# In each weight chunk, all products with the high part first, then those with the low part

## The chip, the cores and the metric

The kernel runs on one core of a Trainium2 chip. The time is the device time of one execution in microseconds (us): three runs of the kernel before gave 1134.96, 1135.42 and 1135.75, so the median is 1135.42. One more execution was profiled; its own time was 1134.29, and its span from first to last instruction 1132.6.

## The reference

One layer on x of 256 tokens by 2048 channels: RMS norm, one wide input projection (2048 by 18,544), a Mamba-2 branch (causal convolution, chunked scan, gated group norm), a sparse-attention branch (index scores, top 64 keys of each query, softmax attention with 16 heads of 128), a projection of each branch back to 2048, merging by sigmoid gates, one output projection, the residual sum and a final norm. In its core:

```
proj = rmsnorm(x) @ w_in
y_m = ssd_branch(z, xbc, dt, ...)          # scan over chunks of 64 tokens
y_a = dsa_branch(q, k, v, gate, qi, ki, wi)
merged = g_m * (y_m @ w_branch[:2048]) + g_a * (y_a @ w_branch[2048:])
out = rmsnorm(x + merged @ w_out)
```

Nearly all of the arithmetic lies in the three weight matrices.

## The kernel before, in words

The weights come in 192 chunks of 128 by 2048 float32 (1 MB each), in the order in which they are used. For each chunk `fetch` issues one DMA on SyncE into a `raw` buffer, ScalarE copies it to `hi` in the reduced float32 format of TensorE (fp32r; line 130), and VectorE computes `lo = raw - hi` (line 131). There are three buffers each of raw, hi and lo, and the chunk two ahead of the one in use is fetched while one is consumed, so a new `hi` or `lo` can be written only when TensorE has finished with the chunk three earlier. The activations are split in the same way.

A product of a weight and an activation is then three products: high by high, high by low, low by high. There are two kinds of units.

- T units (`gemm_t`, 46 after the start, two chunks each) hold the weight still and stream the activations. A chunk has 8 blocks of 128 rows and two column blocks. `high` streams 512 columns (high and low activations side by side), `low` streams the 256 high ones. `chunk_t` goes through the 8 blocks: two `high`, two `low`, and so on. A flag, `lo_last`, makes it all `high` first, then all `low`; only the two units at the very start (`acc_start`) set it, since their data come in pieces.
- N units (`gemm_n`, four chunks each) hold the activations still and stream 512 weight columns, for each of two token blocks: three products for each of 4 blocks of rows (lines 202, 203, 204).

Between chunks `tick` lets earlier work go on that needs small matrix products on TensorE: `prs` (sums for a norm), `prt` and `pcb` (a broadcast, and C times B of the scan), `px`, `py`, `pi` (index scores, four tiles of PSUM, `pi0` to `pi3`), `pl` (attention logits) and `po` (values). In the scan part, groups g = 0 to 3, `u` and `c` are the convolution's tiles, `bc` its result on ScalarE (line 406), `E` the decay matrices (relu at line 427, exp at 428), `dgy` a diagonal (line 483) for which GpSimd raises `ss` to a power (line 480). In the attention part `qT` is the scaled query block (lines 189 and 194).

The program text doesn't fix the order on each engine: the framework schedules the instructions by its own estimates of their times, and each engine then executes its list strictly in that order. PSUM tiles of the small products come from a pool of four.

Of the kernel before, what the change touches and what calls it, by code (L numbers as in the profile page):

```python
# [21 lines left out]
KB = 16  # L22
# [62 lines left out]
def block_kernel(ctx, tc, W, w0, xT, xn, par, gbias, nf, out):  # L85
    nc = tc.nc
    mm = nc.tensor.matmul
# [10 lines left out]
    def acc_tile(name):  # L98

        return pacc.tile([P, 2, 512], F32, tag="acc", name=name)  # L100
# [13 lines left out]
    def tick():  # L114
        state["done"] += 1
        while True:
            due = [p for p in pending if p[0] <= state["done"]]
            if not due:
                return
            for p in due:  # L120
                pending.remove(p)
                p[1]()

    def w_tiles():
        return (wraw.tile([P, 2048], F32, tag="raw", name="raw"),
                whi.tile([P, 2048], F32R, tag="hi", name="hi"),
                wlo.tile([P, 2048], F32R, tag="lo", name="lo"))

    def split(hi, lo, raw):
        nc.scalar.activation(hi, raw, AF.Copy)  # L130
        nc.vector.tensor_sub(lo, raw, hi.bitcast(F32))  # L131
# [15 lines left out]
    def next_chunk():  # L147
        while len(ready) < 1 + AHEAD and state["chunk"] < NCHUNK - 4:
            fetch()
        return ready.pop(0)  # L150

    def chunk_t(acc, hi, lo, half, ks, ax, lo_last=False):

        hv = hi.rearrange("p (k b c) -> p k b c", k=8, b=2)
        lv = lo.rearrange("p (k b c) -> p k b c", k=8, b=2)

        def high(k, cb):
            kk = half * 8 + k
            mm(acc[:, cb, :], hv[:, k, cb], ax[:, kk].rearrange("p b t -> p (b t)"), start=kk == 0, stop=False,  # L159
               skip_group_check=True)  # L160

        def low(k, cb):
            kk = half * 8 + k
            mm(acc[:, cb, 0:T], lv[:, k, cb], ax[:, kk, 0, :], start=False, stop=kk == KB - 1,  # L164
               skip_group_check=True)

        for part_ks in ([ks] if lo_last else [[k] for k in ks]):
            for f in (high, low):
                for k in part_ks:
                    for cb in range(2):  # L170
                        f(k, cb)

    def gemm_t(ax):

        assert UNITS[state["unit"]][0] == "T"
        state["unit"] += 1
        acc = acc_tile("acc_t")
        for half in range(2):
            hi, lo = next_chunk()
            chunk_t(acc, hi, lo, half, range(8), ax)  # L180
            if half == 0:
                tick()
        return acc
# [9 lines left out]
        evict_sum(out, acc)  # L193
        nc.vector.tensor_mul(out, out, rbc2)

    def chunk_n(acc, hi, lo, q, tb, ah, al, c=slice(0, 512)):
        hv = hi.rearrange("p (k c) -> p k c", k=4)
        lv = lo.rearrange("p (k c) -> p k c", k=4)
        ts = slice(tb * P, tb * P + P)
        for k in range(4):  # L200
            kk = q * 4 + k
            mm(acc[:, c], ah[:, kk, ts], hv[:, k, c], start=kk == 0, stop=False)  # L202
            mm(acc[:, c], al[:, kk, ts], hv[:, k, c], start=False, stop=False)  # L203
            mm(acc[:, c], ah[:, kk, ts], lv[:, k, c], start=False, stop=kk == KB - 1)  # L204

    def gemm_n(ah, al):

        assert UNITS[state["unit"]][0] == "N"
        state["unit"] += 1
        both = acc_tile("acc_n")  # L210
        acc = [both[:, tb, :] for tb in range(2)]
        for q in range(4):
            hi, lo = next_chunk()
            for tb in range(2):
                chunk_n(acc[tb], hi, lo, q, tb, ah, al)
            if q < 3:
                tick()
        return acc


    part = const.tile([P, NPAR], F32, name="part")
# [8 lines left out]
    xx = acts.tile([P, KB, 2, T], F32R, name="xx")  # L230
# [4 lines left out]
    k0, k1 = PIECES[0]  # L235
# [8 lines left out]
    acc_start = [acc_tile(f"acc_start{u}") for u in range(2)]  # L244
    for k0, k1 in PIECES:
        ks = slice(k0, k1)
        if k0 % 8 == 0:
            wt = [w_tiles() for u in range(2)]
        ws = slice(256 * (k0 % 8), 256 * (k0 % 8) + 256 * (k1 - k0))
        if k0 > 0:  # L250
            nc.sync.dma_start(xraw[:, ks, :], xTv[:, ks, :])
        for u in range(2):
            nc.sync.dma_start(wt[u][0][:, ws], W[2 * u + k0 // 8][:, ws])
        for k in range(k0, k1):
            g = part[:, PN + k:PN + k + 1]
            nc.scalar.activation(xh[:, k, :], xraw[:, k, :], AF.Copy, scale=g)
            nc.vector.scalar_tensor_tensor(xl[:, k, :], xraw[:, k, :], g, xh[:, k, :].bitcast(F32),
                                           ALU.mult, ALU.subtract)
        for u in range(2):
            raw, hi, lo = wt[u]  # L260
            split(hi[:, ws], lo[:, ws], raw[:, ws])
        for u in range(2):
            raw, hi, lo = wt[u]
            chunk_t(acc_start[u], hi, lo, k0 // 8, range(k0 % 8, k0 % 8 + k1 - k0), xx, True)
    state["unit"], state["chunk"] = 2, 4
    ssm = ExitStack()
    grp = ssm.enter_context(tc.tile_pool(name="grp", bufs=1))
# [6 lines left out]
    raw, hi, lo = w_tiles()  # L274
# [6 lines left out]
    hv = hi[:, :nw].rearrange("p (k c) -> p k c", c=112)  # L281
    lv = lo[:, :nw].rearrange("p (k c) -> p k c", c=112)
# [44 lines left out]
    m0, dt, al, R, rmask = (d2[:, i, :] for i in range(5))  # L327
# [175 lines left out]
    def project_v(j, out):  # L503
        acc = gemm_n(xh, xl)
        for tb in range(2):
            nc.scalar.activation(out[:, tb, :], acc[tb], AF.Copy, scale=rn[:, tb:tb + 1])
# [12 lines left out]
    for g in range(4):  # L519
# [18 lines left out]
        for a in range(2):  # L538
            acc = gemm_t(xx)
# [40 lines left out]
    for j in range(4):  # L580
        acc = gemm_t(xx)
# [35 lines left out]
    for j in range(4):  # L617
        js = slice(512 * j, 512 * j + 512)
        acc = gemm_n(xh, xl)
        tick()  # L620
        if j == 0:
            assert not pending
            select()
            ssm.close()
            late = ctx.enter_context(tc.tile_pool(name="late", bufs=1))
            big = ctx.enter_context(tc.tile_pool(name="big", bufs=1))
            merged = late.tile([P, 2, D], F32, name="merged")
            phase = ExitStack()
            tmp = phase.enter_context(tc.tile_pool(name="att", bufs=2))
        sg = tmp.tile([P, 2, 512], F32, tag="sg", name="sgm")  # L630
        gates(acc, 512 * j, sg)
        acc = gemm_n(yh, yl)
        for tb in range(2):
            nc.vector.tensor_mul(merged[:, tb, js], acc[tb], sg[:, tb, :])
        tick()
# [48 lines left out]
    for j in range(8):  # L684
        kq = []
        for name in ("kT", "qT"):
            acc = gemm_t(xx)
# [15 lines left out]
        acc = gemm_t(xx)  # L703
# [7 lines left out]
    for j in range(4):  # L711
        acc = gemm_n(xh, xl)
# [21 lines left out]
    for j in range(4):  # L734
        js = slice(512 * j, 512 * j + 512)
        acc = gemm_n(yh, yl)
# [19 lines left out]
    for j in range(4):  # L756
# [3 lines left out]
        if j < 3:  # L760
# [4 lines left out]
            acc = gemm_n(mh, ml)  # L765
# [9 lines left out]
    for tb in range(2):  # L775
        r = rf[:, tb:tb + 1]

        nc.vector.tensor_reduce(r, sf[:, tb, 0:3], axis=mybir.AxisListType.X, op=ALU.add)
        nc.vector.tensor_scalar(r, r, 1.0 / D, EPS, ALU.mult, ALU.add)

        n = 512 if tb == 0 else 256
        xs = tmp.tile([P, 512], F32, tag="mt", name="xs")
        for i in range(512 // n):
            acc = acc_tile("acc_last")[:, 0, :]
            c = slice(n * i, n * i + n)
            for q in range(4):
                chunk_n(acc, *ready[q], q, tb, mh, ml, c)
            ps = sf[:, tb, 3 + i:4 + i]
            residual(acc[:, c], 1536 + n * i, 1536 + n * i + n, tb, xr[:, tb, c], ps)

            nc.vector.tensor_mul(xs[:, c], x1[:, tb, 1536 + n * i:1536 + n * i + n], nfb[:, 1536 + n * i:1536 + n * i + n])
            nc.gpsimd.tensor_scalar(r, ps, 1.0 / D, r, ALU.mult, ALU.add)
        nc.gpsimd.tensor_tensor(r, r, mhalf[:, 0:1], op=ALU.pow)
        for i, js in enumerate(slice(512 * i, 512 * i + 512) for i in range(4)):
            o = x1[:, tb, js] if i < 3 else xs
            if i == 1:
                nc.scalar.activation(o, o, AF.Copy, scale=r)
            else:
                nc.vector.tensor_scalar(o, o, r, None, ALU.mult)
            (nc.sync, nc.scalar)[i % 2].dma_start(outv[:, tb, js], o)  # L800
# [54 lines left out]
```

## Time and profile before

| what | value |
|---|---|
| median of three runs | 1135.42 us |
| profiled execution: its time, its span | 1134.29 us, 1132.6 us |
| TensorE busy | 1122.6 us (99%), 5906 matmul records |
| TensorE weight loads busy | 956.8 us (84%) |
| VectorE, ScalarE busy | 779.9 us (69%), 560.3 us (49%) |
| mean granted TensorE clock | 0.998 of full speed |

PE is TensorE, PEld its weight loads (which overlap the products), DVE VectorE, ACT ScalarE, POOL GpSimd, SP SyncE. A matmul's record lasts longer than the distance to the next one, since matmuls are pipelined: what a matmul costs is read from the distance between the starts. A float32 matmul that isn't of the reduced format stands in the trace as two records.

### The profile page before, as it was taken

The page shows a single profiled execution, that of the slowest core. Times are in us where ns is not written, and L with a number is a line of the kernel's source. Part 1 is how long each engine was busy: PE and PEld are TensorE (multiplying, and loading weights), DVE is VectorE, ACT ScalarE, POOL GpSimd, SP SyncE. Part 2 cuts the span into 40 slices and gives each one's busy share as a digit, 9 for nine tenths or more (in the row PEclk, how much of TensorE's full clock was granted, in tenths as well). Part 3 has the DMA queues.
Part 4 walks back from the last instruction along what each step waited for, and adds up shares of the span by engine and source line. Part 5 has one row for each costly group of instructions (what it writes and reads, how often), then busy time and mean ns, then how long its engine had stood idle before and what let it go on. Part 6 is the DMA issues. An engine that isn't in the chain of part 4 may idle for free.

```text
span 1132.6 us, 14323 instructions
## 1 busy us (share of the span) xinstructions
PE 1122.6 (99%) x5906; PEld 956.8 (84%) x5906; DVE 779.9 (69%) x995; ACT 560.3 (49%) x532; POOL 8.8 (1%) x24
## 2 busy tenths in 40 slices
PE   9999999999999999999999999999999999999997
PEld 8888888888888888888888888888888888888886
DVE  6688897879777854454447767877678454889663
ACT  6647675748454433433335454555445444333441
POOL 0000000000000000000000000000000000000000
PEclk9999999999999999999999999999999999999999
DMA  8956555554535655655555454545545567465652
GB/s 294 338 181 229 186 203 176 196 206 150 193 141 187 212 196 187 202 204 207 186 186 186 149 190 183 185 144 192 186 155 181 195 201 271 172 220 186 212 197 75
DMA packets 34113, 219.08 MB, mean 193 GB/s; under 512 B 3744, under 2 KB 3968, under 8 KB 9088
## 3 DMA queue, kind: packets, MB, share of 16 engines
q1 hardware_dynamic: 31392, 209.42, 52.2%
q10 hardware_dynamic: 2656, 8.75, 2.3%
q8 instruction: 46, 0.75, 0.3%
q14 instruction: 19, 0.16, 0.0%
HBM read 215.96 MB, written 2.13 MB: 193 GB/s over the span
## 4 chain that ended last, share of the span: by engine, by line
PE 98%; DMA 1%; ACT 0%; DVE 0%; POOLq 0%; DVEq 0%; issue 0%; POOL 0%
PE acc_t L159 30%; PE acc_t L164 15%; PE acc_n L203 15%; PE acc_n L202 15%; PE acc_n L204 15%; PE acc_start L159 1%; PE py L457 1%; PE acc_last L204 1%; PE acc_last L203 1%; PE acc_last L202 1%; DMA raw<-W 1%; PE pl L650 1%; PE po L678 1%; PE pi L567 1%; PE acc_start L164 1%; PE pl L649 0%
## 5 line engine op out<-in xcount | busy, mean ns | idle before, releaser
L131 DVE TENSOR_TENSOR lo<-raw,hi 128x2048 fp32r<-128x2048 f32 (+2 forms) x197 | 437.7, 2222 | 239.8 <-ACT hi L130 237.3
L130 ACT ACTIVATE hi<-raw 128x2048 fp32r<-128x2048 f32 (+2 forms) x197 | 366.3, 1861 | 455.2 <-PE acc_n L203 222.0
L159 PE MATMUL acc_t<-xx,hi 128*128 128x512 f32 x1472 | 466.6, 398 | 0.0
L164 PEld LDWEIGHTS acc_t<-xx,lo 128*128 128x128 f32 x1472 | 276.3, 188 | 65.1
L164 PE MATMUL acc_t<-xx,lo 128*128 128x256 f32 x1472 | 289.8, 278 | 0.0
L159 PEld LDWEIGHTS acc_t<-xx,hi 128*128 128x128 f32 x1472 | 225.0, 189 | 2.6 <-issue 1.7
L202 PE MATMUL acc_n<-hi,xx 128*128 128x512 f32 x480 | 186.9, 389 | 0.0
L203 PE MATMUL acc_n<-hi,xx 128*128 128x512 f32 x480 | 186.9, 389 | 0.0
L204 PE MATMUL acc_n<-lo,xx 128*128 128x512 f32 x480 | 186.8, 389 | 0.0
L203 PEld LDWEIGHTS acc_n<-hi,xx 128*128 128x128 f32 x480 | 90.1, 188 | 18.8 <-issue 0.3
L204 PEld LDWEIGHTS acc_n<-lo,xx 128*128 128x128 f32 x480 | 90.1, 188 | 18.7
L202 PEld LDWEIGHTS acc_n<-hi,xx 128*128 128x128 f32 x480 | 90.1, 188 | 18.5
L202 PE MATMUL acc_n<-hi,yh 128*128 128x512 f32 x256 | 99.6, 389 | 0.0
L203 PE MATMUL acc_n<-hi,yl 128*128 128x512 f32 x256 | 99.6, 389 | 0.0
L204 PE MATMUL acc_n<-lo,yh 128*128 128x512 f32 x256 | 99.6, 389 | 0.0
L204 PEld LDWEIGHTS acc_n<-lo,yh 128*128 128x128 f32 x256 | 48.1, 188 | 10.0
L203 PEld LDWEIGHTS acc_n<-hi,yl 128*128 128x128 f32 x256 | 48.1, 188 | 10.0
L202 PEld LDWEIGHTS acc_n<-hi,yh 128*128 128x128 f32 x256 | 48.1, 188 | 9.9
L670 DVE STREAM_TRANSPOSE pT<-le 32x192 f32<-32x192 f32 x128 | 47.3, 370 | 1.9
L404 DVE SCALAR_TENSOR_TENSOR c<-u,part,c 128x255 f32<-128x255 f32 (+2 forms) x72 | 30.4, 479 | 0.5
L729 DVE STREAM_TRANSPOSE mT<-merged 32x256 f32<-32x256 f32 x64 | 27.9, 436 | 0.8
L159 PE MATMUL acc_start<-xx,hi 128*128 128x512 f32 x64 | 16.6, 396 | 1.2 <-ACT hi L130 1.0
(199 smaller groups left out, 732.1 us busy)
## 6 DMA issues: line engine op xcount, KB each, us to landing
raw<-W SPq DMA_DIRECT2D x188, 1024.0 KB, 4.8
acb<-adr ACTq DMA_DIRECT2D x4, 1024.0 KB, 4.6
raw<-W SPq DMA_DIRECT2D x6, 512.0 KB, 7.7
xt<-xn SPq DMA_DIRECT2D x2, 1024.0 KB, 5.5
gb<-gbias SPq DMA_DIRECT2D x8, 256.0 KB, 3.5
xr<-xn ACTq DMA_DIRECT2D x4, 512.0 KB, 5.2
xraw<-xT SPq DMA_DIRECT2D x3, 512.0 KB, 6.1
raw<-W SPq DMA_DIRECT2D x4, 256.0 KB, 4.5
```

The lines of the kernel that those rows point to most:

```text
L130: nc.scalar.activation(hi, raw, AF.Copy)
L131: nc.vector.tensor_sub(lo, raw, hi.bitcast(F32))
L159: mm(acc[:, cb, :], hv[:, k, cb], ax[:, kk].rearrange("p b t -> p (b t)"), start=kk == 0, stop=False, skip_group_check=True)
L164: mm(acc[:, cb, 0:T], lv[:, k, cb], ax[:, kk, 0, :], start=False, stop=kk == KB - 1, skip_group_check=True)
L202: mm(acc[:, c], ah[:, kk, ts], hv[:, k, c], start=kk == 0, stop=False)
L203: mm(acc[:, c], al[:, kk, ts], hv[:, k, c], start=False, stop=False)
L204: mm(acc[:, c], ah[:, kk, ts], lv[:, k, c], start=False, stop=kk == KB - 1)
L404: nc.vector.scalar_tensor_tensor(c[:, b, sh:], u[:, b, :T - sh], wv[3 - sh], c[:, b, sh:], ALU.mult, ALU.add)
L457: mm(py[r, cb, sb * P:], xdt[:, sb, 64 * h:64 * h + 64], M[a][:, 2 * cb + i, (0, T)[sb]:(T, 384)[sb]], start=cb == 0 and sb == 0, stop=cb ...
L567: mm(pi[2 * cb + i][:, cs[tb]], qi[r, cb, tb * P:tb * P + P], kidx[r, :(P, T)[tb]], start=tb == 0, stop=tb == 1, skip_group_check=True, ti ...
L670: nc.vector.transpose(t[sj, :, :, si], lv[si, :, :, sj])
L729: nc.vector.transpose(tv[sn, :, :, si], mv[si, :, :, sn])
```

## The change

`chunk_t` loses the flag, and every T chunk has its 16 `high` first and then its 16 `low`. `chunk_n` can do one part alone, and `gemm_n` calls it four times for each chunk: high part for both token blocks, then low part for both. The last unit calls `chunk_n` without a part; there the order inside each call is 8 high, 4 low. Products and their number are the same.

```diff
-        for part_ks in ([ks] if lo_last else [[k] for k in ks]):
-            for f in (high, low):
-                for k in part_ks:
-                    for cb in range(2):
-                        f(k, cb)
+        for f in (high, low):
+            for k in ks:
+                for cb in range(2):
+                    f(k, cb)
...
-        for k in range(4):
-            kk = q * 4 + k
-            mm(acc[:, c], ah[:, kk, ts], hv[:, k, c], start=kk == 0, stop=False)
-            mm(acc[:, c], al[:, kk, ts], hv[:, k, c], start=False, stop=False)
-            mm(acc[:, c], ah[:, kk, ts], lv[:, k, c], start=False, stop=kk == KB - 1)
+        if part != "low":
+            for k in range(4):
+                kk = q * 4 + k
+                mm(acc[:, c], ah[:, kk, ts], hv[:, k, c], start=kk == 0, stop=False)
+                mm(acc[:, c], al[:, kk, ts], hv[:, k, c], start=False, stop=False)
+        if part != "high":
+            for k in range(4):
+                kk = q * 4 + k
+                mm(acc[:, c], ah[:, kk, ts], lv[:, k, c], start=False, stop=kk == KB - 1)
...
-            for tb in range(2):
-                chunk_n(acc[tb], hi, lo, q, tb, ah, al)
+            for part in ("high", "low"):
+                for tb in range(2):
+                    chunk_n(acc[tb], hi, lo, q, tb, ah, al, part=part)
```

Because the framework schedules by its estimates, other instructions move too. On TensorE, in the unit with the second block of index scores, this stands before (`lo_2705` is the end of a chunk, `hi_2779` the start of the next; "waits" names the engines on which an instruction waits):

```order
L164 MATMUL acc_t_2820<-xx_89,lo_2705 128x256 x2
L490 MATMUL prt_2859<-dgy_2747,ones_80 128x128 [waits Activation_49]
L490 MATMUL prt_2859<-dgy_2747,ones_80 128x128
L567 MATMUL pi0_2870<-kidx_408,qi_2816 128x128 [waits DVE_49,Activation_49]
L567 MATMUL pi1_2871<-kidx_408,qi_2816 128x128 [waits Activation_49]
L567 MATMUL pi0_2870<-kidx_408,qi_2816 128x256
L567 MATMUL pi1_2871<-kidx_408,qi_2816 128x256
L567 MATMUL pi2_2872<-kidx_408,qi_2816 128x128 [waits Activation_49]
L567 MATMUL pi2_2872<-kidx_408,qi_2816 128x256
L159 MATMUL acc_t_2820<-xx_89,hi_2779 128x512
L567 MATMUL pi3_2873<-kidx_408,qi_2816 128x128 [waits DVE_49,PE_49]
L567 MATMUL pi3_2873<-kidx_408,qi_2816 128x256
```

and this in the changed kernel (its lines 572 and 495 are 567 and 490 of before):

```order
L159 MATMUL acc_t_2820<-xx_89,hi_2704 128x512 x16
L164 MATMUL acc_t_2820<-xx_89,lo_2705 128x256 x16
L495 MATMUL prt_2859<-dgy_2747,ones_80 128x128 [waits PE_49,Activation_49]
L495 MATMUL prt_2859<-dgy_2747,ones_80 128x128 [waits Activation_49]
L572 MATMUL pi0_2870<-kidx_408,qi_2816 128x128 [waits DVE_49]
L572 MATMUL pi1_2871<-kidx_408,qi_2816 128x128 [waits Activation_49]
L572 MATMUL pi0_2870<-kidx_408,qi_2816 128x256
L572 MATMUL pi1_2871<-kidx_408,qi_2816 128x256
L572 MATMUL pi2_2872<-kidx_408,qi_2816 128x128 [waits Activation_49]
L572 MATMUL pi3_2873<-kidx_408,qi_2816 128x128 [waits Activation_49]
L572 MATMUL pi2_2872<-kidx_408,qi_2816 128x256
L572 MATMUL pi3_2873<-kidx_408,qi_2816 128x256
```

The one `high` product that stood between the products of `pi2` and those of `pi3` has moved behind the group, which is now in one piece and in the order of the other three groups.

On ScalarE, ahead of `bc` of group 1, this stands before, from the eviction of the unit (`u`) on:

```order
L188 ACTIVATE u_1138<-acc_t_1032 128x512 [waits PE_49]
L130 ACTIVATE hi_1156<-raw_1155 128x2048 [waits DMAHW1_49]
L427 ACTIVATE E_1260<-E_1260 128x1536 [waits DVE_49]
L401 ACTIVATE c_1141<-u_1138,part_78 128x256 [waits DVE_49]
L401 ACTIVATE c_1141<-u_1138,part_78 128x256
L428 ACT_TABLE_LOAD
L428 ACTIVATE E_1260<-E_1260 128x1536 [waits Activation_49]
L130 ACTIVATE hi_1203<-raw_1202 128x2048 [waits DMAHW2_49,PE_49]
L406 ACT_TABLE_LOAD [waits DVE_49]
L406 ACTIVATE bc_1142<-c_1141 128x512 [waits Activation_49]
L483 ACTIVATE dgy_1199<-ident_84,ss_1196 128x128 [waits Pool_49]
L483 ACTIVATE dgy_1199<-ident_84,ss_1196 128x128
```

and this in the changed kernel, behind the same `u` (whose row is left off):

```order
L432 ACTIVATE E_1260<-E_1260 128x1536 [waits DVE_49]
L432 ACTIVATE E_1266<-E_1266 128x1536 [waits DVE_49]
L130 ACTIVATE hi_1203<-raw_1202 128x2048 [waits DMAHW2_49,PE_49]
L406 ACTIVATE c_1141<-u_1138,part_78 128x256 [waits DVE_49]
L406 ACTIVATE c_1141<-u_1138,part_78 128x256
L488 ACTIVATE dgy_1199<-ident_84,ss_1196 128x128 [waits Pool_49]
L488 ACTIVATE dgy_1199<-ident_84,ss_1196 128x128
L433 ACT_TABLE_LOAD
L433 ACTIVATE E_1260<-E_1260 128x1536 [waits Activation_49]
L433 ACTIVATE E_1266<-E_1266 128x1536 [waits Activation_49]
L411 ACT_TABLE_LOAD [waits DVE_49]
L411 ACTIVATE bc_1142<-c_1141 128x512 [waits Activation_49]
```

Both halves of `E` and the diagonal `dgy` now stand ahead of `bc`; the split `hi_1156` has moved ahead of `u`.

On TensorE, the product that reads `bc` stands in the third unit after `bc`'s own. Before:

```order
L159 MATMUL acc_t_1154<-xx_89,hi_1101 128x512 x2
L164 MATMUL acc_t_1154<-xx_89,lo_1102 128x256 x2
L159 MATMUL acc_t_1272<-xx_89,hi_1156 128x512 [waits PE_49,Activation_49]
L159 MATMUL acc_t_1272<-xx_89,hi_1156 128x512
L412 MATMUL pcb_1255<-bc_1142 128x256 [waits Activation_49]
L413 MATMUL pcb_1255<-bc_1142 128x128
```

and in the changed kernel:

```order
L164 MATMUL acc_t_1154<-xx_89,lo_1102 128x256 x16
L159 MATMUL acc_t_1272<-xx_89,hi_1156 128x512 [waits Activation_49]
L159 MATMUL acc_t_1272<-xx_89,hi_1156 128x512 x9
L417 MATMUL pcb_1255<-bc_1142 128x256 [waits Activation_49]
L418 MATMUL pcb_1255<-bc_1142 128x128
L159 MATMUL acc_t_1272<-xx_89,hi_1156 128x512 x6
```

`pcb` stood behind 2 `high` products of its unit and now stands behind 10. Groups 2 and 3 have the same moves; in group 0 `pcb` stays at the end of a chunk.

## Rows read from the trace of the kernel before

**Rows 1.** The page: shares of the span in the chain that ended last.
```profile
PE 98%; DMA 1%; ACT 0%; DVE 0%; POOLq 0%; DVEq 0%; issue 0%; POOL 0%
```
**Rows 2.** Timeline, PE, units of the start (start us, us, engine, line, xcount).
```profile
23.91 2.00 PE L159 MATMUL acc_start<-xx,hi 128*128 128x512 f32 x8
25.75 1.12 PE L164 MATMUL acc_start<-xx,lo 128*128 128x256 f32 x8
26.71 2.00 PE L159 MATMUL acc_start<-xx,hi 128*128 128x512 f32 x8
```
**Rows 3.** Timeline, PE, starts of two chunks of T units, two chunks between them.
```profile
578.48 0.63 PE L159 MATMUL acc_t<-xx,hi 128*128 128x512 f32 x2
...
595.20 0.63 PE L159 MATMUL acc_t<-xx,hi 128*128 128x512 f32 x2
```
**Rows 4.** Timeline, PE, last unit: 40 matmuls, then 90, between these rows.
```profile
1104.07 0.39 PE L204 MATMUL acc_last<-lo,xx 128*128 128x512 f32 x1
...
1113.13 0.28 PE L202 MATMUL acc_last<-hi,xx 128*128 128x256 f32 x1
...
1123.93 0.28 PE L202 MATMUL acc_last<-hh,xx 128*128 128x256 f32 x1
```
**Rows 5.** Timeline, PE, first and second group of index scores.
```profile
319.14 1.58 PE L567 MATMUL pi<-kidx,qi 64*128 64x128 f32 x16
320.65 0.73 PE L159 MATMUL acc_t<-xx,hi 128*128 128x512 f32 x2
...
332.44 1.57 PE L567 MATMUL pi<-kidx,qi 64*128 64x128 f32 x12
...
335.23 0.50 PE L159 MATMUL acc_t<-xx,hi 128*128 128x512 f32 x1
```
**Rows 6.** Timeline, ACT, DVE and PE, one block of attention logits (idle before <-releaser).
```profile
667.68 1.92 ACT L130 ACTIVATE hi<-raw 128x2048 fp32r<-128x2048 f32 x1 [3.65 <-PE acc_t L159]
669.63 2.29 DVE L131 TENSOR_TENSOR lo<-raw,hi 128x2048 fp32r<-128x2048 f32 x1 [3.28 <-ACT hi L130]
672.56 0.69 DVE L194 TENSOR_TENSOR qT<-qT,rbc 128x512 f32<-128x512 f32 x1
673.01 0.40 PE L164 MATMUL acc_t<-xx,lo 128*128 128x256 f32 x2
673.31 0.49 PE L649 MATMUL pl<-kT,qT 128*128 128x128 f32 x2
673.63 0.60 PE L650 MATMUL pl<-kT,qT 128*128 128x256 f32 x2
674.07 0.38 PE L649 MATMUL pl<-kT,qT 128*128 128x128 f32 x2
674.29 0.60 PE L650 MATMUL pl<-kT,qT 128*128 128x256 f32 x2
```
**Rows 7.** Timeline, PE, DVE, POOL and ACT, around bc of group 1.
```profile
135.11 0.50 PE L477 MATMUL prs<-ones,sz 128*128 128x1 f32 x4
141.13 0.63 PE L159 MATMUL acc_t<-xx,hi 128*128 128x512 f32 x2
...
137.24 0.14 DVE L479 TENSOR_SCALAR ss<-prs 128x2 f32<-128x2 f32 x1
...
137.46 1.08 POOL L480 TENSOR_TENSOR ss<-ss,mhalf 128x2 f32<-128x2 f32 x1 [92.12 <-DVE ss L479]
...
135.80 1.49 ACT L428 ACTIVATE E<-E 128x1536 f32<-128x1536 f32 x1
139.12 1.28 ACT L406 ACT_TABLE_LOAD   x1
140.41 0.64 ACT L406 ACTIVATE bc<-c 128x512 f32<-128x512 f32 x1
140.95 0.68 ACT L483 ACTIVATE dgy<-ident,ss 128x128 f32<-128x128 f32 x2
```

More of the change, by code (lines that the diff above doesn't have):

```diff
@@ L150, in next_chunk, with chunk_t @@
         return ready.pop(0)
-    def chunk_t(acc, hi, lo, half, ks, ax, lo_last=False):
+    def chunk_t(acc, hi, lo, half, ks, ax):
         hv = hi.rearrange("p (k b c) -> p k b c", k=8, b=2)
@@ L194, in evict_t, with chunk_n @@
         nc.vector.tensor_mul(out, out, rbc2)
-    def chunk_n(acc, hi, lo, q, tb, ah, al, c=slice(0, 512)):
+    def chunk_n(acc, hi, lo, q, tb, ah, al, c=slice(0, 512), part=None):
         hv = hi.rearrange("p (k c) -> p k c", k=4)
@@ L263, in block_kernel @@
             raw, hi, lo = wt[u]
-            chunk_t(acc_start[u], hi, lo, k0 // 8, range(k0 % 8, k0 % 8 + k1 - k0), xx, True)
+            chunk_t(acc_start[u], hi, lo, k0 // 8, range(k0 % 8, k0 % 8 + k1 - k0), xx)
     state["unit"], state["chunk"] = 2, 4
```

## The prediction

> **What bounds the kernel now.** I read the page's shares of the chain that ended last first. The chain is TensorE for 98% [rows 1]. So the time is the sum of the distances between TensorE's matmul starts, and only two things can move it: what a matmul costs by its place in the order, and the few places where TensorE stands still for a small product. ScalarE and VectorE matter only where their order makes a small product late. Next I read the timeline of TensorE for the distances, and then, around each kind of small product, the timeline of the engines that feed it.
>
> I call a product of 512 columns with the high part H and one of 256 columns with the low part L. After the start there are 46 T units of two chunks, so 92 T chunks, each with 16 H and 16 L: 1472 of each.
>
> **Term 1: the order of H and L, 92 chunks.** Before, a chunk is 8 times H H L L. One chunk starts at 578.48 and the third after it at 595.20, so a chunk takes 16.72 / 3 = 5.573 us [rows 3]. The new order is in the trace already, in pieces of half the length: the units of the start run 8 H and then 8 L. The H take 25.75 - 23.91 = 1.84 us, the L 0.96, together 2.80 [rows 2]. Two such pieces would be 5.60. But a chunk will have one long piece of each and not two short ones. In a long run the distances settle: 40 matmuls of 512 columns in the last unit take 1113.13 - 1104.07 = 9.06 us, which is 0.2265 each, and 90 of 256 columns take 10.80, which is 0.120 each [rows 4]. The first 8 H after L are thus 1.84 - 8 x 0.2265 = 0.03 above the settled rate, and they pay that once in a chunk. So a chunk will take 1.84 + 8 x 0.2265 + 0.96 + 8 x 0.120 = 5.57 us. These rows are rounded to 0.01 and leave a gain of 0 to 0.015 for each chunk; I take 0.007 from the middle. Times 92 this is -0.6 us. The bounds: at the settled rates throughout, 16 x (0.2265 + 0.120) = 5.544, it would be -2.7 us; if the slow H after a run of L grow with the run's length (0.03 more in each chunk), about +2. I take -0.6, since the trace shows both run lengths next to it.
>
> [...]
>
> N units: all their products have 512 columns, in either order, and the settled 0.2265 holds for all three kinds [rows 4]. I cost that edit at nothing. The first token block's sum is now complete only 4 products before the second's instead of 12. VectorE and ScalarE read it outside TensorE's path, since the next unit writes the other accumulator.
>
> **Term 2: one split group of index scores.** The first group of `pi` takes from 319.14 to 320.65, 1.51 us. In the second, one H stands between `pi2` and `pi3`, and the group takes from 332.44 to 335.23, 2.79 us, with that one H of 0.23 in it [rows 5]. The price of the split is 2.79 - 1.51 - 0.23 = 1.05 us. The new order has the group in one piece: -1.05 us. The third and fourth groups were whole already. Bounds: 0 if `pi3` then waits for its buffer, and -1.05.
>
> **Term 3: attention logits, 8 times.** `pl` waits for `qT`. `qT` ends at 672.56 + 0.69 = 673.25 and `pl` starts at 673.31 [rows 6]. The two L ahead of it started at 673.01, and two L take 0.24 (8 take 0.96 [rows 2]), so `pl` could have started at 673.25: 0.06 late. Its first pair takes 673.63 - 673.31 = 0.32, the same pair of the second head 674.29 - 674.07 = 0.22: the late weight load costs another 0.10. Together 0.16 us, 8 times, 1.3 us.
>
> What makes `qT` late is a buffer. The split `hi` at 667.68 waited 3.65 us for TensorE's last H of a chunk; `lo` at 669.63 waited for that `hi`; `qT` stands behind that `lo` on VectorE [rows 6]. In the new order the last H of a chunk is followed by 16 L (1.92 us) instead of 2, so this `hi` can start about 1.7 us earlier. The `lo` has its own buffer to wait for, freed by the last L at the chunk's end, which is about 667.9. It starts there instead of at 669.63, and `qT` is ready at about 671.5. What is late next is nothing: `pl` follows the chunk at once. -1.3 us; bounds 0 and -1.3.
>
> **Term 4: `pcb` of groups 1 to 3.** ScalarE's new list puts both `E` and `dgy` ahead of `bc`, and TensorE's list puts `pcb` 8 H later. I follow it with group 1's rows [rows 7]. `dgy` needs `ss`, and that needs `prs`, whose place on TensorE stays: 135.11 + 0.50 = 135.61. In the old list VectorE came to `ss` only at 137.24, in the new one `ss` stands before a `lo`, so VectorE takes it at once, at 135.65. GpSimd starts 137.46 - 137.24 = 0.22 after that and takes 1.08: 136.95. The eviction, the two relus, the split and `c` are done by about 136.3 by their durations, so ScalarE waits for GpSimd. Then `dgy` 0.68, a table load 1.28, two exps of 1.49, a table load 1.28, `bc` 0.64: 6.86 us, so `bc` is there at 143.81. TensorE starts its unit at 141.13 and reaches `pcb` after 10 H: 1.84 + 2 x 0.2265 = 2.29, so at 143.42. It waits 0.4 us, in three groups 1.2 us. What is queued behind `pcb` is the whole of TensorE, so all of it counts. Bounds: 0, if GpSimd's rough duration is too long by 0.4; and if everything added to the list (a relu and an exp of 1.49 and `dgy`, 3.7 us) came out in full against the 8 H (1.85) and the old slack of 0.5 (`bc` ended at 141.05, and `pcb` stood two H after 141.13), 1.3 us three times, +4. I take +1.2.
>
> Everything else hides. The splits were ready ahead of need, and L is needed 3.6 us later in each chunk than before, while `hi` buffers come free earlier. The DMAs and their number stay. ScalarE has fewer table loads. In the attention part a `lo` now stands ahead of the softmax on VectorE, which delays `po`'s input by about 2 us, but `po` comes a unit and a half later on TensorE.
>
> **The sum** is -0.6 - 1.05 - 1.3 + 1.2 = -1.75 us, from 1134.29 to 1132.54 for the profiled execution. That execution was 1.13 below the median of the runs, so for the median I say 1135.42 - 1.75 = 1133.7.
>
> **Rivals.**
> - `bc` is in time (Term 4 is zero). For it: my chain rests on GpSimd's span, which the profile calls rough, and the framework put `pcb` where its estimates have `bc` ready; before, `bc` came 0.5 ahead. Against it: the durations add up to a wait. The time: 1135.42 - 2.95 = 1132.5, faster.
> - The early release buys nothing (Terms 2 and 3 vanish, one because a `pi` tile waits for its buffer, the other because `qT` still waits on VectorE). For it: `lo` keeps its release at the chunk's end. Against it: that end is 1.7 us before `lo`'s old start. The time: -0.6 + 1.2, 1136.0, same.
> - Slower: long runs of L settle worse than 0.120. Its place is all 92 chunks, and its price is 1.47 us for each ns (1472 L). With the other terms at -1.75 it is slower than before from 0.1212, and by over 2.27 us from 0.1227. For it: the H after 8 L are slower (0.230) than the settled 0.2265, so runs of L leave something behind. Against it: 90 matmuls of 256 columns in a row kept 0.120. At 0.124 the time is 1133.7 + 5.9 = 1139.6.
>
> **How the numbers follow.** My forecast, 1133.7, has a chance of 0.55, with its own range of 1132.8 to 1134.8. `bc` in time has 0.25, nothing bought 0.13, slower runs 0.07. What can be told from no change is 0.2%, 2.27 us: below 1133.15 is faster, above 1137.69 slower. Faster: all of the second case and 0.07 of the forecast, 0.32. Slower: the last case, most of it, 0.06. Same: 0.62. The range that holds 8 in 10 takes in `bc` in time and nothing bought: 1131.9 to 1136.3. The bounds of all terms together would reach from about 1130 to 1140, which needs four errors of one sign.
>
> **What would show it.** Right: a T chunk of 5.57 us between starts; H at 0.227 in the second half of its run and L at 0.120; the second `pi` group whole, 1.51 us; `pl` starting 0.12 after the last L, with pairs of 0.22; a wait of TensorE of 0.4 us before `pcb` of groups 1 to 3, released by `bc`. Wrong: a T chunk off by more than 0.02; `pcb` without a wait; a new wait on `hi`, `lo` or an accumulator.

## The result and the profile after

The changed kernel takes 1143.91 us (six runs, 1142.31 to 1145.56), the kernel before beside it 1135.35 (six runs, 1134.96 to 1135.75). The ratio is 1.0076, with an interval of 1.0066 to 1.0085: slower by 8.6 us, where 1133.7 was predicted. The profiled execution of the changed kernel took 1142.31, its span 1140.6.

The page after, shares of the span in the chain that ended last, to be held against [rows 1]:

```profile
PE 94%; DMA 2%; ACT 2%; POOL 1%; DVE 0%; issue 0%; SPq 0%; POOLq 0%; DVEq 0%; ACTq 0%
```

TensorE has lost four hundredths of the chain to ScalarE, GpSimd and transfers. So the path now runs through engines that were off it. The waits of TensorE by line, in us in total, times, and the longest (other waits of the start left out):

```profile
PE pcb L417 <- ACT bc L411: 5.8, 3, 2.0
...
PE pi L572 <- ACT rl L577: 0.8, 2, 0.4
PE acc L291 <- DVE lo L131: 0.6, 1, 0.6
```

Most of it is one wait, three times: `pcb` waits for `bc`. The timeline after around `bc` of group 1, to be held against [rows 7] (TensorE, VectorE, GpSimd, ScalarE):

```profile
142.10 2.46 PE L159 MATMUL acc_t<-xx,hi 128*128 128x512 f32 x10
146.46 0.70 PE L417 MATMUL pcb<-bc 128*128 128x256 f32 x2 [1.90 <-ACT bc L411]
...
136.63 0.16 DVE L484 TENSOR_SCALAR ss<-prs 128x2 f32<-128x2 f32 x1 [1.40 <-PE prs L482]
136.71 2.29 DVE L131 TENSOR_TENSOR lo<-raw,hi 128x2048 fp32r<-128x2048 f32 x1
...
136.87 2.69 POOL L485 TENSOR_TENSOR ss<-ss,mhalf 128x2 f32<-128x2 f32 x1 [91.30 <-DVE ss L484]
...
139.59 0.69 ACT L488 ACTIVATE dgy<-ident,ss 128x128 f32<-128x128 f32 x2 [2.29 <-POOL ss L485]
140.30 1.28 ACT L433 ACT_TABLE_LOAD   x1
141.60 2.86 ACT L433 ACTIVATE E<-E 128x1536 f32<-128x1536 f32 x2
144.48 1.28 ACT L411 ACT_TABLE_LOAD   x1
145.77 0.63 ACT L411 ACTIVATE bc<-c 128x512 f32<-128x512 f32 x1
```

The chain is the one the prediction drew: `ss`, the power on GpSimd, `dgy`, a table load, two exps, a table load, `bc`. What differs is one row. GpSimd takes 2.69 us where [rows 7] have 1.08, and ScalarE stands for 2.29 us ahead of `dgy`. Note how to read it: the wait is put down to ScalarE's `bc`, but ScalarE is busy from `dgy` on; its own only idle time ends with GpSimd.

After the third of these waits something more happens. Windows of the changed kernel: length, busy time of PE, PEld, DVE, ACT and POOL, then the granted clock, DMA share and GB/s:

```profile
270.70:273.90 3.20, 1.21 (x7) 0.74 (x7) 0.32 (x1) 3.17 (x5) 0.00 (x0) 1.00 0.00 0
273.90:278.00 4.10, 4.10 (x19) 3.57 (x18) 4.10 (x5) 3.12 (x2) 0.00 (x0) 0.58 0.00 0
278.00:282.00 4.00, 4.00 (x25) 3.49 (x24) 3.90 (x8) 1.81 (x4) 0.00 (x0) 1.00 0.00 0
```

The first window holds the wait, at the full clock. In the second the mean granted clock is 0.58: for most of it TensorE ran at 1.2 GHz instead of 2.4, with 427 ns between the starts of products of 512 columns and 213 between those of 256. I call such a stretch a spell of the half clock.

Where the 8 us went is seen best by the starts of the same chunk in two profiles. I take the kernel before profiled once more (below, the run `before_again`), whose start is like the changed one's. Start of a chunk after minus before:

| stretch | difference grows by |
|---|---|
| start, to the first N product | -0.03 us |
| groups 1 and 2, at `pcb` | 2.17 and 2.14 |
| group 3, at `pcb` | 3.78 (2.15 for the wait, 1.63 for the half clock) |
| first and second group of index scores | 0.83 and -0.17 |
| eight blocks of attention logits, together | -1.31 |
| all other T chunks together | -0.5 |
| N chunks | 0.00 |
| sum, by the last product | 6.93 |

The spans differ by the same, 1140.6 - 1133.7 = 6.9. The median is 1.6 higher than the profiled execution, and I put that down to the half clock too, by a sum: without any spell the time would be 1142.31 - 1.63 = 1140.7, and each spell adds 1.63, so 1142.3, 1143.9 and 1145.6 for one, two and three. The six runs read 1142.31, 1143.65, 1143.69, 1144.14, 1144.51 and 1145.56, and the mean granted clock is 0.997 in the first and 0.994 in the last. Where the spells of the five runs without a profile lie is not recorded, so this is worked out and not seen. Three profiles with these waits (this one and two below) stand in the same order: 1140.45 without a spell, 1142.31 with one, 1144.40 with two.

### The profile page after: what moved, and what is told of

The parts are those of the page before. It is cut to its first block, busy times and chain, and to the rows that moved or that the text cites. A ratio compares the mean times of both kernels' runs of the same rounds, so it can differ in the third digit from the quotient of the medians.

```text
span 1140.6 us, 14306 instructions
## 1 busy us (share of the span) xinstructions
PE 1123.2 (98%) x5906; PEld 961.6 (84%) x5906; DVE 778.6 (68%) x995; ACT 559.8 (49%) x526; POOL 13.8 (1%) x24
## 4 chain that ended last, share of the span: by engine, by line
PE 94%; DMA 2%; ACT 2%; POOL 1%; DVE 0%; issue 0%; SPq 0%; POOLq 0%; DVEq 0%; ACTq 0%
PE acc_t L159 28%; PE acc_t L164 15%; PE acc_n L202 15%; PE acc_n L203 15%; PE acc_n L207 15%; DMA xraw<-xT 1%; PE py L462 1%; DMA raw<-w 1%; POOL ss L485 1%; PE acc_last L207 1%; PE acc_last L203 1%; PE acc_last L202 1%; PE pl L655 1%; PE po L683 1%; PE pi L572 1%; ACT E L433 1%
## 5 line engine op out<-in xcount | busy, mean ns | idle before, releaser
L159 PE MATMUL acc_t<-xx,hi 128*128 128x512 f32 x1472 | 357.4, 395 | 0.0
L159 PEld LDWEIGHTS acc_t<-xx,hi 128*128 128x128 f32 x1472 | 271.1, 188 | 55.3 <-issue 1.7
L164 PEld LDWEIGHTS acc_t<-xx,lo 128*128 128x128 f32 x1472 | 189.5, 192 | 7.3
L164 PE MATMUL acc_t<-xx,lo 128*128 128x256 f32 x1472 | 191.6, 283 | 0.0
L207 PE MATMUL acc_n<-lo,xx 128*128 128x512 f32 x480 | 118.5, 389 | 0.0
L207 PE MATMUL acc_n<-lo,yh 128*128 128x512 f32 x256 | 63.2, 389 | 0.0
L662 ACT ACTIVATE le<-le,st 128x128 f32<-128x128 f32 (+1 forms) x32 | 14.2, 445 | 10.2 <-DVE st L658 10.2
```

The lines of the kernel that those rows point to most:

```text
L662: nc.scalar.activation(le[:, c], le[:, c], AF.Exp, scale=-1.0, bias=st[:, tb:tb + 1], accum_out=st[:, 2 + tb:3 + tb])
```

## The experiments

**Which half of the edit does it.** One kernel has the new order in the T chunks alone, one in the N chunks alone.

```
t_only:  chunk_t as after, chunk_n and gemm_n as before
n_only:  chunk_n and gemm_n as after, chunk_t as before
```

> The new order in the T chunks only, the N chunks as before. Theory A (the T order makes the scheduler put dgy and both E exponentials ahead of bc on ScalarE; TensorE then waits about 2.05 us for bc in groups 1 to 3, and the clock falls after one to three of these waits): the same three waits with the same releaser and 1142.3 to 1145.6 us. Theory B (the N order costs time, by the later eviction of the first token block): no waits at pcb and about 1133.5 to 1135.5 us.

> The new order in the N chunks only, the T chunks as before. Theory A: ScalarE's list keeps bc ahead of dgy, no wait at pcb, the split index-score group and the late qT stay as before: 1135.4 us, within 0.3. If the extra 0.8 us at the start is of the N edit: 1136.2. Theory B: 1140 us or more.

Measured: the T order alone 1143.98 us (1142.14 to 1145.67; ratio 1.0075, 1.006 to 1.009), with the three waits (2.06, 2.06 and 2.15 us by the starts of the products). Its profiled execution took 1144.40 and has two spells of the half clock, after the second and third waits: group 2 costs 3.69 and group 3 3.78 us, group 1 2.17. The N order alone 1135.59 (1135.11 to 1136.0; ratio 1.0002, 0.9992 to 1.0012), with no wait at `pcb`. Theory B has fallen. The N edit costs nothing and brings nothing.

**Is it `dgy` ahead of `bc`?** One edge more in the changed kernel, so that ScalarE gets `dgy` behind `bc`; both exps stay ahead.

```
-        nc.scalar.activation(o, c, AF.Silu)
+        ins = nc.scalar.activation(o, c, AF.Silu)
+        if name == "bc":
+            state["bc"] = ins.ins
...
-        for tb in range(2):
-            nc.scalar.activation(dgy[:, tb * P:tb * P + P], ident, AF.Copy, scale=ss[:, tb:tb + 1])
+        with tc.issue_after(state["bc"]):
+            for tb in range(2):
+                nc.scalar.activation(dgy[:, tb * P:tb * P + P], ident, AF.Copy, scale=ss[:, tb:tb + 1])
```

> The changed kernel with one edge more: dgy is issued behind bc on ScalarE; both E exponentials stay ahead of bc. Theory A (GpSimd's 2.66 us is what holds bc back): bc ends about 143.3 us where TensorE reaches pcb at 143.9, so no wait at pcb, no half clock, three times 2.05 and 1.6 us less than the profiled 1142.3: 1134.5 in the profile, 1134.3 to 1135.5 as the median; the runs agree within 0.8 us, since no spell of the half clock is left. Rival C (bc is late because of the exponentials, GpSimd or not): waits of 0.4 us or more stay, 1136 to 1139.

Measured: 1134.48 us (ten runs, 1133.9 to 1134.8), ratio 0.9991 (0.9981 to 1.0). The timeline around `bc` of group 1 with this edge (GpSimd, ScalarE, TensorE):

```profile
137.46 2.69 POOL L487 TENSOR_TENSOR ss<-ss,mhalf 128x2 f32<-128x2 f32 x1 [90.50 <-DVE ss L486]
...
139.21 2.86 ACT L435 ACTIVATE E<-E 128x1536 f32<-128x1536 f32 x2
...
143.39 0.63 ACT L411 ACTIVATE bc<-c 128x512 f32<-128x512 f32 x1
...
142.69 2.00 PE L159 MATMUL acc_t<-xx,hi 128*128 128x512 f32 x8
144.54 0.59 PE L419 MATMUL pcb<-bc 128*128 128x256 f32 x2
```

GpSimd still takes 2.69 us, but nothing waits for it. `bc` ends at 144.02, half a microsecond before `pcb`, and `pcb`, which here stands behind 8 H, starts with no wait. 9.4 us of the median are gone, and with them the spread of 3 us between runs. Rival C (the exps alone make `bc` late) has fallen in the form in which it was put: with both exps still ahead `bc` is in time.

**What makes GpSimd slow.** A chain of 151 more of these powers, beside the N units:

```
+        if j == 0:
+            pch = const.tile([P, 2], F32, name="pch")
+            nc.gpsimd.tensor_tensor(pch, sg[:, 0, 0:2], mhalf, op=ALU.pow)
+            for _ in range(150):
+                nc.gpsimd.tensor_tensor(pch, pch, mhalf, op=ALU.pow)
```

> The changed kernel with a chain of 151 more pow operations (128x2, on a tile of their own) on GpSimd, beside the N units in which VectorE mostly does lo, an operation with two inputs in SBUF. Theory A (GpSimd can't work while VectorE does such an operation): a pow that falls in VectorE's idle time takes 0.7 to 1.1 us, one during which or before which a lo begins takes up to about 2.7 to 3 us and ends with or just after that lo. Rival (the 2.66 us of groups 1 to 3 are GpSimd's own, from a long pause or from what ran before): the first pow of the chain is long and all others take one same time, whatever VectorE does.

Timeline of VectorE and GpSimd in that kernel, where one `lo` begins in the chain (x2 are two powers with their gap):

```profile
460.83 2.29 DVE L131 TENSOR_TENSOR lo<-raw,hi 128x2048 fp32r<-128x2048 f32 x1 [3.15 <-ACT hi L130]
...
459.84 1.46 POOL L641 TENSOR_TENSOR pch<-pch,mhalf 128x2 f32<-128x2 f32 x2
...
461.38 2.29 POOL L641 TENSOR_TENSOR pch<-pch,mhalf 128x2 f32<-128x2 f32 x1
...
463.75 0.69 POOL L641 TENSOR_TENSOR pch<-pch,mhalf 128x2 f32<-128x2 f32 x1
```

The power at 461.38 begins while the `lo` runs and ends at 463.67, 0.55 after the `lo` (460.83 + 2.29 = 463.12). It is the same for all: 32 of the 151 begin while a `lo` runs, take 2.2 to 2.77 us, and end 0.55 us after it; the other 119 take 0.69, also those beside VectorE operations that read an accumulator in PSUM. Theory A holds for a power behind a `lo`. Its other half is a miss: 27 `lo` began during a power, and these powers took 0.69 like the rest. The end of the `lo` plus 0.55 us also gives the changed kernel's row (136.71 + 2.29 + 0.55 = 139.55, GpSimd ends at 139.56). In the kernel before, VectorE was doing a shorter addition of `E` there, and the same sum gives the 1.08 of [rows 7]:

```profile
137.31 0.67 DVE L424 TENSOR_TENSOR E<-acb,nat 128x512 f32<-128x512 f32 x1
```

That is 137.31 + 0.67 + 0.55 = 138.53, and 137.46 + 1.08 = 138.54. The powers of `ss` in all ten profiles agree. Of the first three in each kernel, 29 of 30 begin inside a VectorE operation on two tiles in SBUF (`lo`, the addition of `E`, or `c`) and end 0.54 to 0.56 us after it; the other one takes 0.69. Of the ten fourth powers, four take 0.69, and six end 0.55 us after an operation on one tile (`sc`, 0.35 us), so two tiles are not the only case. The Trainium skill's page "SBUF — State Buffer", section "Who interferes with whom", has a rule for this: a VectorE operation with two inputs in SBUF and a GpSimd operation that reads SBUF exclude each other, and the one issued second waits. The trace agrees for a power behind a `lo`. For the other order no run here shows a wait of VectorE: the 27 `lo` that began inside a power, 0.13 us or more after its start, took 2.28 or 2.29 us like nearly all others in the chain's stretch.

**The second exp behind `bc` instead.**

```
-            nc.scalar.activation(E, E, AF.Relu, scale=-1.0)
-            nc.scalar.activation(E, E, AF.Exp, scale=-1.0)
+            if a == 0 or g == 0:
+                nc.scalar.activation(E, E, AF.Relu, scale=-1.0)
+                nc.scalar.activation(E, E, AF.Exp, scale=-1.0)
+            else:
+                with tc.issue_after(state["bc"]):
+                    nc.scalar.activation(E, E, AF.Relu, scale=-1.0)
+                    nc.scalar.activation(E, E, AF.Exp, scale=-1.0)
```

> The changed kernel with the second E's relu and exp behind bc, dgy still ahead of it. The scheduler then puts pcb at the head of the unit, and in groups 1 and 2 no exponential ahead of bc. By theory A's sums on ScalarE: groups 1 and 2 have dgy done about 1.8 us before the unit begins and then only bc: a wait of 0 to 0.3 us; group 3 has dgy, a table load, an exp, a table load and bc (0.69 + 1.28 + 1.43 + 1.28 + 0.63 = 5.3 us after GpSimd): a wait of about 2.8 us, with or without a spell of the half clock. Time 1136.5 to 1138.7. Rival C (GpSimd doesn't matter, the exponentials do): the same without group 3's wait of more than 1.5 us.

Measured: 1134.79 us in one run, and no wait at `pcb` in any group. The 2.8 us forecast for group 3 is a miss: the scheduler moved more than the edge asked for. It put the `hi` and `lo` that ran beside the power behind `dgy` (in all three groups), and in group 3 an exp with its table load ahead of `c`. The timeline of VectorE, GpSimd, ScalarE and TensorE in group 1 there:

```profile
137.09 0.47 DVE L409 SCALAR_TENSOR_TENSOR c<-u,part,c 128x255 f32<-128x255 f32 x1
...
137.25 0.87 POOL L492 TENSOR_TENSOR ss<-ss,mhalf 128x2 f32<-128x2 f32 x1 [91.39 <-DVE ss L491]
...
138.16 0.70 ACT L495 ACTIVATE dgy<-ident,ss 128x128 f32<-128x128 f32 x2 [1.41 <-POOL ss L492]
140.56 0.61 ACT L411 ACTIVATE bc<-c 128x512 f32<-128x512 f32 x1
...
142.49 0.60 PE L419 MATMUL pcb<-bc 128*128 128x256 f32 x2
```

With no `lo` beside it the power takes 0.87 us here, 0.86 in group 2 and 0.69 in group 3, and `dgy` ahead of `bc` is harmless. The 0.87 comes out of the sum above with the shorter operation `c`: 137.09 + 0.47 + 0.55 = 138.11, and the power ends at 138.12. But since the order moved too, this run doesn't by itself tell GpSimd's share from that of the exps.

**What a stop of TensorE costs beyond its length.** Ten made stops in the N units of the changed kernel, with n from 1 to 16 copies; the later N products stand behind the product that reads the copies.

```
+        with tc.issue_after(state["mm"].ins):
+            m = mm(sp[:, 0:2], ones, mhalf, start=True, stop=True)
+        nc.scalar.activation(t[:, 0:2], sp[:, 0:2], AF.Copy)
+        for _ in range(n):
+            nc.scalar.activation(t, t, AF.Copy)
+        with tc.issue_after(m.ins):
+            m = mm(sp[:, 2:4], ones, t[:, 0:2], start=True, stop=True)
...
+            with tc.issue_after(state["behind"]) if "behind" in state else ExitStack():
```

> The changed kernel with ten made stops of TensorE in the N units: a small product, a chain of 1, 2, 3, 4, 5, 6, 8, 10, 12 and 16 copies on ScalarE, a small product that reads it, and all later products behind that one. It prices a stop. Theory A1 (a stop of about 2 us or more can drop the granted clock to 1.2 GHz for a few us, at about 1.6 us more): after the longest stops the distances go to about 427 ns for some 3.6 us, after the stops under 1 us they stay at 227. Rival (the half clock in the changed kernel had nothing to do with the stop): all stops leave the distances at 227 and cost only their own length.

The tenth stop didn't come about (a T chunk went into it). The timeline at four of the nine others, TensorE, with the idle time ahead of the reading product:

```profile
448.67 0.38 PE L222 MATMUL sp<-hold,ones 128*128 128x2 f32 x2 [1.41 <-ACT hold L220]
...
472.78 0.38 PE L222 MATMUL sp<-hold,ones 128*128 128x2 f32 x2 [1.70 <-ACT hold L220]
...
498.78 0.38 PE L222 MATMUL sp<-hold,ones 128*128 128x2 f32 x2 [1.99 <-ACT hold L220]
...
523.75 0.38 PE L222 MATMUL sp<-hold,ones 128*128 128x2 f32 x2 [2.57 <-ACT hold L220]
```

And the windows behind these four (columns as above, the granted clock third from the end):

```profile
449.00:453.00 4.00, 4.00 (x19) 3.29 (x19) 0.65 (x1) 0.14 (x1) 0.00 (x0) 1.00 0.57 176
473.00:477.00 4.00, 4.00 (x13) 3.16 (x13) 0.42 (x1) 0.00 (x0) 0.00 (x0) 0.58 0.57 201
499.00:503.00 4.00, 4.00 (x20) 3.31 (x20) 0.18 (x1) 0.04 (x1) 0.00 (x0) 1.00 0.68 231
524.00:528.00 4.00, 4.00 (x13) 3.19 (x13) 0.00 (x0) 0.00 (x0) 0.00 (x0) 0.61 0.75 262
```

By the distances of product starts, the four shortest stops (0.80 to 1.66 us) leave the clock at 2.4 GHz. The fifth (1.95) drops it, the sixth (2.24) does not, and the three longest (2.82, 3.39, 3.96) drop it. Each spell costs about 1.6 us in longer distances (every stop also has one distance of 315 ns right behind it, 0.09 us), about what group 3 paid (1.63). Theory A1 holds, with one thing to add: near 2 us a stop may or may not cost this. So may the waits at `pcb`: of three like waits one is followed by a spell in the changed kernel's profile, two in the T-only kernel's, two in the kernel with the made stops, and none in that with the chain of powers (1140.45 us), so five of twelve.

**Is the late start of the change?** The kernel before, profiled again.

```
before_again:  no edit
```

> The kernel before once more, for its start. In the first profile the first N product starts at 35.13 us; in the changed kernel at 36.12. If the 1.0 us is of the start's transfers and not of the change: 36.0 to 36.8 here, with a wait of 0.5 to 0.9 us for lo of w0, at a span of 1133.4 to 1133.9. If it is of the change: 35.1 again.

Measured: 1135.40 us, span 1133.7; TensorE at its start:

```profile
30.67 0.37 PE L286 MATMUL acc<-xx,lo 128*112 128x256 f32 x1 [0.48 <-DVE lo L131]
36.16 0.40 PE L202 MATMUL acc_n<-hi,xx 128*128 128x512 f32 x1
```

So the wait for `lo` of `w0` is also in the kernel before. The execution that the prediction worked from had an early start, the earliest of the ten profiles; the 1.0 us is not of the change. In the kernel with the chain of powers, which has the change, the first N product starts at 35.48.

**A version that beats both.** The edge of `pin_dgy`, and the first two groups of index scores half a unit later, away from `prs` and `prt`:

```
-        after(2, lambda j=j, qi=qi: index_scores(j, qi))
+        after(3 if j < 2 else 2, lambda j=j, qi=qi: index_scores(j, qi))
```

> The kernel with dgy behind bc, and the first two groups of index scores half a unit later, so that they no longer stand next to prs and prt. Expected: each pi group whole, 1.51 us, and pi3 waits for nothing that is late; against the kernel with dgy behind bc alone 0.66 + 1.05 = 1.7 us less, so 1134.5 - 1.7 = 1132.8 us, which beats the kernel before by 2.5 us. If pi3's wait only moves to another buffer, 1133.7 to 1134.5.

Measured: 1132.63 us (nine runs, 1132.19 to 1133.03) against 1135.67 of the kernel before beside it (13 runs, 1135.15 to 1136.26): ratio 0.9973, 0.9963 to 0.9983. TensorE, the first two groups there:

```profile
325.59 1.58 PE L575 MATMUL pi<-kidx,qi 64*128 64x128 f32 x16
327.10 3.96 PE L159 MATMUL acc_t<-xx,hi 128*128 128x512 f32 x16
...
338.93 1.58 PE L575 MATMUL pi<-kidx,qi 64*128 64x128 f32 x16
340.44 3.96 PE L159 MATMUL acc_t<-xx,hi 128*128 128x512 f32 x16
```

Both take 1.51 us, as forecast. Against the kernel before, this version has what the new order was able to give, without what it set off.

## Why the prediction was wrong

**Term 1, the order of H and L: right.** T chunks in the timeline of the changed kernel, to be held against [rows 3]:

```profile
587.99 3.82 PE L159 MATMUL acc_t<-xx,hi 128*128 128x512 f32 x16
...
602.78 2.08 PE L164 MATMUL acc_t<-xx,lo 128*128 128x256 f32 x16
604.69 1.55 PE L159 MATMUL acc_t<-xx,hi 128*128 128x512 f32 x6
```

Three chunks take 16.70 us, 5.567 each; forecast 5.57. Together about -0.5, forecast -0.6. Long runs of L kept 0.120 (16 in 604.69 - 602.78 = 1.91): the slower rival is out. N units: 0.00.

**Term 3, attention logits: right.** The block of [rows 6] in the changed kernel (ScalarE, VectorE, TensorE):

```profile
675.13 1.91 ACT L130 ACTIVATE hi<-raw 128x2048 fp32r<-128x2048 f32 x1 [3.65 <-PE acc_t L159]
...
680.00 0.69 DVE L193 TENSOR_TENSOR qT<-qT,rbc 128x512 f32<-128x512 f32 x1
...
680.45 2.07 PE L164 MATMUL acc_t<-xx,lo 128*128 128x256 f32 x16
682.36 0.39 PE L654 MATMUL pl<-kT,qT 128*128 128x128 f32 x2
682.58 0.60 PE L655 MATMUL pl<-kT,qT 128*128 128x256 f32 x2
```

`qT` is ready at 680.69, 1.7 us ahead of need, and `pl` follows 16 L (1.91) at once, with 0.22 for its first pair. Eight times, -1.31 us; forecast -1.3.

**Term 2, index scores: wrong by its sign.** Forecast -1.05 with a bound of 0, "if `pi3` then waits for its buffer". It does, and so does the first group's, which was whole before. TensorE after, to be held against [rows 5]:

```profile
328.01 1.14 PE L572 MATMUL pi<-kidx,qi 64*128 64x128 f32 x10
329.50 0.92 PE L572 MATMUL pi<-kidx,qi 64*128 64x128 f32 x6 [0.36 <-ACT rl L577]
330.35 0.96 PE L159 MATMUL acc_t<-xx,hi 128*128 128x512 f32 x3
...
342.13 1.14 PE L572 MATMUL pi<-kidx,qi 64*128 64x128 f32 x10
343.67 0.92 PE L572 MATMUL pi<-kidx,qi 64*128 64x128 f32 x6 [0.41 <-ACT rl L577]
344.52 0.72 PE L159 MATMUL acc_t<-xx,hi 128*128 128x512 f32 x2
```

The groups take 2.34 and 2.39 us where a free one takes 1.51. `prs` or `prt` holds one of the four buffers just ahead of them; the new list gives `pi3` a buffer that ScalarE's `rl` has to free. Before, `pi3` of the first group waited only for VectorE, and that had been done. The two groups cost +0.66 instead of -1.05: 1.7 us off. `pin_pi` shows it from the other side: by the starts of the same chunks, its first two groups take 1.55 us less than those of `pin_dgy` (0.89 less than before, where `pin_dgy` takes 0.66 more).

**Term 4, `pcb`: the step that failed.** Its place, its releaser, its chain and its count were right; its size was not. The prediction took GpSimd's power as 1.08, the row of the kernel before, "GpSimd starts 0.22 after that and takes 1.08". It had itself put `ss` ahead of a `lo` on VectorE in the sentence before, and didn't ask what runs beside GpSimd there. The power took 2.69, since it began behind that `lo`; the wait was not 0.4 but 2.05 (1.6 more), and three waits cost 6.46 us (2.17, 2.14, 2.15) instead of 1.2. That is beyond the bound of +4, which had no room for a slower GpSimd; the only GpSimd case that was weighed was a shorter one. The split of the 2.05 into 0.4 and 1.6 is worked out from the rows; a kernel with the same lists and a free GpSimd was not run.

**What the prediction left out: the clock.** It priced a wait at its length. Each of these can be followed by a spell of 1.2 GHz, 1.63 us more: one in the profiled execution, and two at the median by the sum in the section on the result.

Sum for the median, by these sizes: -0.5 - 1.3 + 0.66 + 6.46 + 2 x 1.63 = +8.6 us; measured 1143.91 - 1135.35 = 8.56. The start of the profiled execution, 1.0 us early, was no part of the error, since the forecast went by the median. The range to 1136.3 and the 0.06 for slower were too narrow for the same reason: the one term with a new wait was bounded by ScalarE's work alone. The upper bounds of all four terms (+2, 0, 0 and +4) make 1141.4 and not the 1140 that the prediction gives, and the measured median lies above that too.

## What to carry to other kernels

When a change lets a scheduler reorder an engine, take no duration of a GpSimd operation from its old place: look at what VectorE runs beside it in the new list, and add what is left of that operation (here the power ended 0.55 us after it). An item that waits for another engine should not stand ahead of the one that TensorE waits for; one edge in the issue order was worth 9.4 us here. And where a change makes TensorE stop for as long as these stops did (1.95 us and more), allow for a spell of the lower clock on top, about 1.6 us here, and for a wider spread between runs.

## What the hardware showed that was not expected

A GpSimd operation on 128x2 elements, 0.69 us alone, takes up to 2.77 when a VectorE subtraction of two SBUF tiles has begun before it, and ends 0.55 us after that subtraction in all 32 cases. A subtraction that begins 0.13 us or more after it leaves both at their usual length (27 cases). Stops of TensorE of 0.80 to 1.66 us left its granted clock at 2.4 GHz; of those from 1.95 to 3.96 us four in five were followed by a spell at 1.2 GHz that cost about 1.6 us each.
